# Depthwise-convolution taps issued between a mixer's attention units and gate blocks, one channel block wholly on Pool; rotary key rows kept in lasting tiles

## The chip, the cores and the metric

The kernel runs on one core of one Trainium2 chip (trn2). The metric is the device time of one execution in microseconds (us). TensorE (PE) multiplies; VectorE (DVE), ScalarE (ACT) and GpSimd (POOL) do everything else between its products; SyncE (SP) issues the weight loads.

## The reference, cut to what matters

The model is a two-layer hybrid block on 256 latent and 256 context tokens with 1024 channels. Each layer is a half-step feed-forward, a mixer, and a second half-step feed-forward. The change touches the mixer alone:

```python
def conv_module(zc, w_dw, b_dw, ln_g, ln_b, w_pw, b_pw):
    a, gt = jnp.split(zc, 2, axis=-1)
    v = a * jax.nn.sigmoid(gt)
    v = lax.conv_general_dilated(v, w_dw[:, None, :], window_strides=(1,),
                                 padding=[(CONV_K // 2, CONV_K // 2)],   # CONV_K = 31
                                 feature_group_count=CONV_CH) + b_dw     # CONV_CH = 384
    v = layer_norm(v, ln_g, ln_b)
    return jax.nn.silu(v) @ w_pw + b_pw
...
# every head's key: its own 64 rows, and 32 rotary rows shared by all 8 heads
k = jnp.concatenate([k_nope, jnp.broadcast_to(kr[:, :, None, :], (bsz, t, N_HEADS, QK_ROPE))], axis=-1)
...
g0, g1, g2 = jnp.split(jax.nn.sigmoid(u @ w_bg + b_bg), 3, axis=-1)
return (g0 * y_conv + g1 * y_mla + g2 * y_four) @ w_out
```

The second layer's mixer needs the latent stream only; its keys and values still come from both streams.

## The kernel before

Channels lie on the 128 partitions and tokens in the columns, latent and context side by side. Mixer 0 (layer 0) works on 512 columns; mixer 1 (the last layer) on 256, its keys on 512. A float32 product is made in three passes (L261 to L263) of split operands: high times high, high times low, low times high. Weights come as 512 KB tiles of 128x1024 on SP's queue into `raw` (3 buffers). ACT casts each to `wh` (L240), DVE subtracts to get the rest `wl` (L241); both have 5 buffers. PE's third pass (L263) is the one that reads `wl`.

A tile scheduler lays each engine's instructions out in program order with priorities, and each engine runs its own list in that order. `issue_after(x)` adds an ordering edge: what is emitted inside stands behind x. Tiles come from one pool by tag, each tag with a number of buffers (`BUFS`); a new tile of a full tag waits until the oldest one is no longer read.

A mixer runs in this order: the input projection; the norms and the rotary key rows (`rope_keys`); attention; the Fourier branch (`project`, `over_tokens`, `over_channels`); then the three branches by their gates, `wf` (Fourier, gate 2), `wo` (attention, gate 1), `pw` (convolution, gate 0), each in 8 output blocks m; then the output projection. One output block of `wf` or `wo` is 8 gate products and 4 branch products of three passes each, 36 matmuls on 12 weight blocks, which is one and a half weight tiles.

Attention goes in units of 128 queries of one head and stream: 32 units in mixer 0 (half of them with 512 keys, half with 256), 16 in mixer 1. For a unit, PE makes the scores, DVE takes the maximum (L762), ACT the exponentials (L765), DVE the reciprocal of their sum (L767), POOL multiplies (L768: the softmax product). PE transposes the unit's probabilities (L780) four units later. Keys are made per pair of heads into a fresh `kq` tile each, and POOL copies the shared rotary rows into it (L815, two copies a head).

The convolution has 31 taps for each of 3 channel blocks. A tap on DVE is one instruction that multiplies and adds (L669). A tap on POOL is two, a product into a scratch tile (L666) and an addition (L667). Before, blocks 0 and 1 run on DVE and block 2 on POOL; in mixer 1 POOL also takes 20 taps of block 1. All stand behind attention, two steps at a time around the parts of the Fourier branch, three per block of `wf`, and the rest at block 2 of `wo`, where the convolution's layer norm (`conv_norm`) starts. POOL's scratch tiles have the tag `hid`, which holds nearly every other 128x512 tile of the mixer too, also the 8 sums of the branches (`macc`), written by L1023.

Of the kernel before, what the change touches and what calls it, by code (L numbers as in the profile page):

```python
# [182 lines left out]
class Kern:  # L183
    def __init__(self, ctx, tc, nc, ap, offs):
        self.tc, self.nc, self.ap, self.offs = tc, nc, ap, offs
        pool = lambda name, bufs, **k: ctx.enter_context(tc.tile_pool(name=name, bufs=bufs, **k))  # noqa: E731
# [193 lines left out]
    def ada_steps(self, todo):  # L380
        """The adaLN vectors (layer, index) of todo, 128 channels a step: a row's products with silu(c), summed."""
        nc = self.nc
        cb = []
# [798 lines left out]
```

## Time and profile before

| | |
|---|---|
| three runs | 2027.84 us median, 2027.41 to 2029.29 |
| profiled execution | span 2026.3 us |
| PE, DVE, ACT, POOL busy | 97%, 64%, 37%, 18% of the span |
| tensor clock granted | 1.00 nearly throughout, less in a few stretches of the two mixers |
| mixer 0: attention, Fourier, `wf` and `wo` | about 477 to 545, 545 to 578, 578 to 700 us |
| mixer 1: the same | about 1611 to 1653, 1653 to 1680, 1680 to 1745 us |

All times of the trace count from the start of the span. What one execution takes beside its span is 1.5 us if the median stands for it. The windows give, for a stretch, how long each engine was busy, how many instructions it ran, and the clock that PE was granted as a share of full speed (2.4 GHz). A wait names the engine that stood still, the line that came next, and what released it.

### The profile page before, as it was taken

What the parts mean: (1) busy time and instruction counts of PE and PEld (TensorE: products, weight loads), DVE (VectorE), ACT (ScalarE), POOL (GpSimd) and SP (SyncE); (2) the same over time, 40 slices, a digit from 0 to 9 for tenths busy, and PEclk for the clock granted to TensorE, in tenths of its full rate; (3) what the DMA queues carried; (4) which work ended last, traced back from release to release, by engine and by line L of the source; (5) the groups of instructions that cost most, each with busy time, mean ns of one, the idle gap of its engine ahead of it and who ended that gap; (6) DMA issues with size and microseconds to landing.
All of it is one profiled execution on the core that took longest, in us unless ns stands there. A gap on an engine that the chain in (4) does not pass through costs nothing.

```text
span 2026.3 us, 27858 instructions
## 1 busy us (share of the span) xinstructions
PE 1971.3 (97%) x10949; PEld 1701.1 (84%) x10949; DVE 1287.2 (64%) x2064; ACT 759.0 (37%) x1171; POOL 361.3 (18%) x417
## 2 busy tenths in 40 slices
PE   7999999999979999999999999999999999899998
PEld 5888888988768888988888898888889878799997
DVE  5667667855698545666755766454456777577674
ACT  4322222345622434422132242222234663455453
POOL 1000000123686000100000010000001389300000
PEclk9999999999999999999999999999999999899999
DMA  9445545420213333444544534454542314465653
GB/s 351 158 163 190 175 158 179 133 94 22 71 42 125 94 104 112 139 151 152 183 159 147 168 120 160 166 187 145 166 141 88 105 60 148 135 198 178 184 181 102
DMA packets 81428, 290.44 MB, mean 143 GB/s; under 512 B 9232, under 2 KB 10512, under 8 KB 81296
## 3 DMA queue, kind: packets, MB, share of 16 engines
q1 hardware_dynamic: 62320, 221.01, 33.0%
q0 software_dynamic: 18432, 67.12, 10.7%
q8 instruction: 86, 1.41, 0.3%
q10 hardware_dynamic: 544, 0.52, 0.1%
q14 instruction: 46, 0.38, 0.1%
HBM read 287.57 MB, written 1.05 MB: 142 GB/s over the span
## 4 chain that ended last, share of the span: by engine, by line
PE 81%; issue 10%; POOL 5%; DVE 3%; ACT 1%; DMA 1%; SPq 0%; POOLq 0%; DVEq 0%; ACTq 0%
PE mm L261 25%; PE mm L263 25%; PE mm L262 25%; POOL hid L666 2%; POOL hid L667 2%; DVE hid L669 1%; PE mm L446 1%; PE mm L793 1%; PE mm L780 1%; PE mm L307 1%; DVE wl L241 1%; PE mm L320 1%; PE mm L939 1%; PE mm L458 0%; DVE hid L289 0%
## 5 line engine op out<-in xcount | busy, mean ns | idle before, releaser
L240 ACT CAST wh<-raw 128x1024 fp32r<-128x1024 f32 x394 | 412.9, 1050 | 1010.5 <-PE mm L262 606.6
L263 PE MATMUL mm<-uh,wl 128*128 128x512 f32 (+2 forms) x2056 | 717.1, 349 | 14.6 <-DVE wl L241 14.6
L261 PE MATMUL mm<-uh,wh 128*128 128x512 f32 (+2 forms) x2056 | 718.8, 350 | 0.0
L262 PE MATMUL mm<-ul,wh 128*128 128x512 f32 (+2 forms) x2056 | 716.9, 349 | 1.2 <-POOL ul L371 1.2
L241 DVE TENSOR_TENSOR wl<-raw,wh 128x1024 fp32r<-128x1024 f32 x394 | 494.2, 1256 | 255.7 <-ACT wh L240 255.2
L263 PEld LDWEIGHTS mm<-uh,wl 128*128 128x128 f32 x2056 | 392.3, 191 | 65.4 <-DVE wl L241 17.0
L262 PEld LDWEIGHTS mm<-ul,wh 128*128 128x128 f32 x2056 | 392.5, 191 | 51.0 <-POOL ul L371 1.4
L261 PEld LDWEIGHTS mm<-uh,wh 128*128 128x128 f32 x2056 | 392.0, 191 | 49.2 <-issue 1.0
L263 PE MATMUL mm<-hid,wl 128*128 128x512 f32 (+1 forms) x1086 | 372.9, 344 | 5.9 <-DVE wl L241 5.9
L261 PE MATMUL mm<-hid,wh 128*128 128x512 f32 (+1 forms) x1086 | 374.0, 344 | 0.0
L262 PE MATMUL mm<-hid,wh 128*128 128x512 f32 (+1 forms) x1086 | 372.8, 343 | 0.0
L398 DVE SCALAR_TENSOR_TENSOR kq<-kq,kq 128x1024 f32<-128x1024 f32 x224 | 273.0, 1219 | 1.3
L263 PEld LDWEIGHTS mm<-hid,wl 128*128 128x128 f32 x1086 | 206.4, 190 | 30.6 <-DVE wl L241 6.7
L261 PEld LDWEIGHTS mm<-hid,wh 128*128 128x128 f32 x1086 | 206.4, 190 | 24.5
L262 PEld LDWEIGHTS mm<-hid,wh 128*128 128x128 f32 x1086 | 206.4, 190 | 24.4
L396 POOL DMA_DIRECT2D kq<-in_ada x128 | 68.1, 532 | 890.3 <-DVE kq L398 804.0
L612 DVE TENSOR_TENSOR tmp<-mm,tmp 128x512 f32<-128x512 f32 (+1 forms) x70 | 46.2, 660 | 195.0 <-PE mm L263 195.0
L522 DVE SCALAR_TENSOR_TENSOR h<-mm,mod,h 128x256 f32<-128x256 f32 x136 | 61.4, 480 | 84.8 <-PE mm L263 84.4
L666 POOL TENSOR_SCALAR hid<-cv,vec,zero 128x251 f32<-128x251 f32 (+29 forms) x80 | 101.1, 1268 | 26.7 <-PE mm L262 15.2
L667 POOL TENSOR_TENSOR hid<-hid,hid 128x251 f32<-128x251 f32 (+29 forms) x80 | 89.2, 1116 | 1.7
L669 DVE SCALAR_TENSOR_TENSOR hid<-cv,vec,hid 128x482 f32<-128x482 f32 (+29 forms) x100 | 83.9, 882 | 0.2
L312 POOL TENSOR_TENSOR r<-ms,mhalf 128x2 f32<-128x2 f32 (+1 forms) x17 | 16.8, 987 | 362.2 <-DVE ms L310 362.2
(176 smaller groups left out, 1514.3 us busy)
## 6 DMA issues: line engine op xcount, KB each, us to landing
raw<-in_w SPq DMA_DIRECT2D x392, 512.0 KB, 4.1
kq<-in_ada POOLq DMA_DIRECT2D x128, 512.0 KB, 3.9
kq<-in_ada_first SPq DMA_DIRECT2D x16, 512.0 KB, 7.7
kq<-in_crow SPq DMA_DIRECT2D x6, 512.0 KB, 6.2
h<-in_xt SPq DMA_DIRECT2D x8, 256.0 KB, 4.1
raw<-in_four SPq DMA_DIRECT2D x2, 384.0 KB, 3.0
out_t<-hid ACTq DMA_DIRECT2D x2, 256.0 KB, 2.3
out_t<-hid SPq DMA_DIRECT2D x2, 256.0 KB, 2.4
```

What stands on the lines that cost most here:

```text
L240: a = nc.scalar.copy(out=wh, in_=raw)
L241: b = nc.vector.tensor_sub(out=wl, in0=raw, in1=wh.bitcast(F32))
L261: nc.tensor.matmul(out, lh, rh, start=k == 0, stop=False)
L262: nc.tensor.matmul(out, lh, rl, start=False, stop=False)
L263: nc.tensor.matmul(out, ll, rh, start=False, stop=k == n - 1)
L396: nc.gpsimd.dma_start(out=raw, in_=self.ap[f"ada{l}"][p - (2 if l == 0 else 0), b])
L398: nc.vector.scalar_tensor_tensor(out=junk, in0=raw, scalar=1.0, in1=cb[s], op0=ALU.mult, op1=ALU.mult, accum_out=m[:, s, b : b + 1])
L522: self.mark = self.nc.vector.scalar_tensor_tensor(out=h[:, cs], in0=ps, scalar=gate[:, s, kb : kb + 1], in1=h[:, cs], op0=ALU.mult, op1=AL ...
L612: self.mark = nc.vector.tensor_tensor(out=t, in0=p3[:, :n], in1=t, op=ALU.mult)
L666: nc.gpsimd.tensor_scalar(out=tmp, in0=src, scalar1=c, scalar2=self.zero, op0=ALU.mult, op1=ALU.add)
L667: nc.gpsimd.tensor_add(out=dst, in0=dst, in1=tmp)
L669: nc.vector.scalar_tensor_tensor(out=dst, in0=src, scalar=c, in1=dst, op0=ALU.mult, op1=ALU.add)
```

## The change

- The taps are two generators now, `near` (blocks 0 and 1, on DVE) and `far` (block 2, on POOL) in both mixers: 62 DVE taps and 31 POOL steps each. The 20 taps of block 1 that POOL had in mixer 1 are DVE's.
- They are called from inside attention by `during(i)`, behind unit i's scores. In mixer 1 each unit gets one DVE tap behind its maximum and one POOL step behind its softmax product. In mixer 0 every fourth unit gets a DVE tap, every second unit a POOL step. The 15 POOL steps left follow the last softmax product at once.
- None stands around the Fourier branch. The DVE taps left go 5 (mixer 0) or 4 (mixer 1) to an output block of `wf` and of `wo`, behind the block's product with its gate; `conv_norm` starts at block 3 or 4 of `wo`.
- POOL's scratch has a tag of its own, `ptmp`, with two buffers.
- `rope_keys` makes four lasting key tiles (`kt`) with the rotary rows in them, by 6 POOL copies ahead of attention; heads use them in turn, and the 16 copies of L815 are gone. `kq` has 4 buffers and not 6; the adaLN steps take their broadcast rows from `kt`. The scratch for POOL's DMA descriptors is set to 4096 bytes.

```diff
-    BUFS = {"hid": 26, "kq": 6, "tmp": 6, "cv": 3, "sq": 6}
+    BUFS = {"hid": 26, "kq": 4, "kt": 4, "tmp": 6, "cv": 3, "sq": 6, "ptmp": 2}
...
-                tmp = grid(self.blk("hid"))[:, :, lo:hi]
+                tmp = grid(self.blk("ptmp"))[:, :, lo:hi]
...
-        help_with = [(2, k) for k in order] + [(1, k) for k in order[late:]]
-        for i, k in enumerate(order):
-            tap(0, k, False)
-            if i < late:
-                tap(1, k, False)
-            while len(help_with) > (CONV_K - 1 - i) * (CONV_K + moved) // CONV_K:
-                tap(*help_with.pop(0), True)
-            yield
+        def steps(blocks, helper):
+            for k in order:
+                for j in blocks:
+                    tap(j, k, helper)
+                    yield
+
+        return steps((0, 1), False), steps((2,), True)
...
+        for to in kt[1:]:
+            for dst, src in zip(to, kr):
+                nc.gpsimd.tensor_scalar(
+                    out=dst[NOPE:], in0=src[NOPE:].bitcast(F32), scalar1=self.one[NOPE:], scalar2=self.zero[NOPE:], op0=ALU.mult, op1=ALU.add
+                )
+        return kt
...
-                kh, kl = self.pair()
+                kh, kl = kt[(2 * pr + hh) % 4]
                 self.split_from(pk[hh * NOPE : (hh + 1) * NOPE], kh[:NOPE], kl[:NOPE])
-                for dst, src in zip((kh, kl), kr):
-                    nc.gpsimd.tensor_scalar(
-                        out=dst[NOPE:], in0=src[NOPE:].bitcast(F32), scalar1=self.one[NOPE:], scalar2=self.zero[NOPE:], op0=ALU.mult, op1=ALU.add
-                    )
...
-        nc.vector.reduce_max(out=nb, in_=ps[:, :nk], axis=mybir.AxisListType.X, negate=True)
+        self.top = nc.vector.reduce_max(out=nb, in_=ps[:, :nk], axis=mybir.AxisListType.X, negate=True)
...
-        nc.gpsimd.tensor_scalar(out=p, in0=p, scalar1=ri, scalar2=self.zero, op0=ALU.mult, op1=ALU.add)
+        self.soft = nc.gpsimd.tensor_scalar(out=p, in0=p, scalar1=ri, scalar2=self.zero, op0=ALU.mult, op1=ALU.add)
...
                 self.scores(u)
+                each(i)
...
+        near, far = self.conv_steps(l, v, conv, ns)
+
+        def taps(n, ins):
+            with self.tc.issue_after(ins):
+                for _ in range(n):
+                    next(near, None)
+
+        per_m, at_m = (4, 4) if last else (5, 3)
+
+        def during(i):
+
+            taps(1 if last else i % 4 // 3, self.top.ins)
+            if last or i % 2:
+                with self.tc.issue_after(self.soft.ins):
+                    next(far, None)
...
+        with self.tc.issue_after(self.soft.ins):
+            for _ in far:
+                pass
...
-        taps(2)
         project(2)
-        taps(2)
         project(3)
-        taps(2)
         spectra = [over_tokens(b) for b in batches]
-        taps(2)
...
-        def normalise(m):
-            if m == 2:
-                taps(100)
+        def normalise(m, ins):
+            if m < at_m:
+                taps(per_m, ins)
+            elif m == at_m:
+                taps(100, ins)
                 self.conv_norm(l, conv, ns, y)
 
-        branch("wf", 2, four, self.vec(l, "b_four"), step=lambda m: taps(3))
+        branch("wf", 2, four, self.vec(l, "b_four"), step=lambda m, ins: taps(per_m, ins))
```

POOL's list at the first units of mixer 0's attention, before: L768 is the softmax product, L815 the copy of rotary rows.

```order
L768 TENSOR_SCALAR tmp_3758<-tmp_3758,ri_3761,zero 128x512
L768 TENSOR_SCALAR tmp_3776<-tmp_3776,ri_3779,zero 128x512
L815 TENSOR_SCALAR kq_3830<-hid_3439,one,zero 64x512
L768 TENSOR_SCALAR sq_3788<-sq_3788,ri_3791,zero 128x256
L768 TENSOR_SCALAR sq_3800<-sq_3800,ri_3803,zero 128x256
L815 TENSOR_SCALAR kq_3830<-hid_3440,one,zero 64x512
L768 TENSOR_SCALAR tmp_3812<-tmp_3812,ri_3815,zero 128x512
```

The same place of the changed kernel, where L774 is the softmax product and L664 with L665 one tap of block 2:

```order
L774 TENSOR_SCALAR tmp_3763<-tmp_3763,ri_3766,zero 128x512
L774 TENSOR_SCALAR tmp_3781<-tmp_3781,ri_3784,zero 128x512
L661 TENSOR_SCALAR hid_3665<-cv_3455,vec_94 128x512
L774 TENSOR_SCALAR sq_3794<-sq_3794,ri_3797,zero 128x256
L774 TENSOR_SCALAR sq_3806<-sq_3806,ri_3809,zero 128x256
L664 TENSOR_SCALAR ptmp_3813<-cv_3455,vec_94,zero 128x2x241
L665 TENSOR_TENSOR hid_3665<-hid_3665,ptmp_3813 128x2x241
L774 TENSOR_SCALAR tmp_3822<-tmp_3822,ri_3825,zero 128x512
```

The copies between the softmax products are gone, and a tap of two instructions stands behind every second product; the product that follows waits on POOL for both.

DVE's list at the last units of mixer 1's attention, before (L762 maximum, L767 reciprocal):

```order
L762 TENSOR_REDUCE nb_13180<-mm_13176 128x1
L762 TENSOR_REDUCE nb_13198<-mm_13194 128x1
L767 RECIPROCAL ri_13185<-sm_13183 128x1
L762 TENSOR_REDUCE nb_13217<-mm_13213 128x1
L767 RECIPROCAL ri_13203<-sm_13201 128x1
L767 RECIPROCAL ri_13222<-sm_13220 128x1
```

And of the changed kernel (L768 maximum, L773 reciprocal, L667 a tap):

```order
L768 TENSOR_REDUCE nb_13201<-mm_13197 128x1
L667 SCALAR_TENSOR_TENSOR hid_12664<-cv_12454,vec_95,hid_12664 128x246
L768 TENSOR_REDUCE nb_13223<-mm_13219 128x1
L773 RECIPROCAL ri_13206<-sm_13204 128x1
L667 SCALAR_TENSOR_TENSOR hid_12663<-cv_12453,vec_95,hid_12663 128x247
L768 TENSOR_REDUCE nb_13246<-mm_13242 128x1
L773 RECIPROCAL ri_13228<-sm_13226 128x1
```

One tap now stands between a unit's maximum and its reciprocal.

DVE's list in mixer 1's Fourier branch, before (L289 takes the low part of a split that PE's next product reads):

```order
L289 TENSOR_TENSOR hid_13390<-mm_13232,hid_13389 128x512
L669 SCALAR_TENSOR_TENSOR hid_13311<-cv_12461,vec_95,hid_13311 128x247
L669 SCALAR_TENSOR_TENSOR hid_13312<-cv_12462,vec_95,hid_13312 128x247
L669 SCALAR_TENSOR_TENSOR hid_13311<-cv_12461,vec_95,hid_13311 128x248
L669 SCALAR_TENSOR_TENSOR hid_13312<-cv_12462,vec_95,hid_13312 128x248
L669 SCALAR_TENSOR_TENSOR hid_13311<-cv_12461,vec_95,hid_13311 128x249
L289 TENSOR_TENSOR kq_13407<-mm_13408,kq_13406 128x512
```

And of the changed kernel, from the Fourier branch into the first block of `wf` (L1034 is the block's product with its gate):

```order
L289 TENSOR_TENSOR hid_13491<-tmp_13486,hid_13490 128x512
L241 TENSOR_TENSOR wl_13662<-raw_13659,wh_13661 128x1024
L289 TENSOR_TENSOR hid_13506<-tmp_13501,hid_13505 128x512
L241 TENSOR_TENSOR wl_13686<-raw_13683,wh_13685 128x1024
L1034 SCALAR_TENSOR_TENSOR hid_13509<-mm_13550,vec_95,tmp_13548 128x256
L667 SCALAR_TENSOR_TENSOR hid_12663<-cv_12453,vec_95,hid_12663 128x248
L667 SCALAR_TENSOR_TENSOR hid_12664<-cv_12454,vec_95,hid_12664 128x248
L667 SCALAR_TENSOR_TENSOR hid_12663<-cv_12453,vec_95,hid_12663 128x249
L667 SCALAR_TENSOR_TENSOR hid_12664<-cv_12454,vec_95,hid_12664 128x249
L241 TENSOR_TENSOR wl_13737<-raw_13734,wh_13736 128x1024
```

No tap stands among the splits any more; they follow a block's own product, four at a time, and the weight splits stand between.

## Rows read from the trace of the kernel before

**Rows 1.** Windows of mixer 0 (Fourier 560, branches 580).

```profile
core 0: us, PE busy (x) PEld busy (x) DVE busy (x) ACT busy (x) POOL busy (x), PEclk, DMA share, GB/s
440.00:460.00 20.00, 20.00 (x90) 16.57 (x89) 8.59 (x10) 7.00 (x9) 4.94 (x4) 1.00 0.35 107
480.00:532.00 52.00, 51.84 (x315) 41.19 (x314) 36.09 (x85) 40.54 (x110) 28.12 (x41) 1.00 0.10 29
560.00:580.00 20.00, 17.72 (x107) 15.33 (x108) 19.62 (x29) 7.02 (x15) 14.16 (x10) 1.00 0.00 1
580.00:620.00 40.00, 32.65 (x124) 25.56 (x123) 40.00 (x36) 8.27 (x9) 39.68 (x24) 0.87 0.31 92
```

**Rows 2.** Windows of mixer 1, same columns.

```profile
1611.00:1646.00 35.00, 33.45 (x207) 26.99 (x207) 24.75 (x55) 26.22 (x62) 22.10 (x26) 1.00 0.09 27
1660.00:1680.00 20.00, 16.50 (x89) 15.20 (x88) 17.02 (x30) 6.66 (x12) 19.84 (x23) 0.74 0.17 49
1680.00:1750.00 70.00, 55.16 (x399) 53.42 (x399) 45.56 (x59) 24.30 (x33) 60.18 (x65) 0.90 0.46 145
1750.00:1790.00 40.00, 40.00 (x335) 39.94 (x334) 28.11 (x49) 22.91 (x35) 1.63 (x1) 1.00 0.56 172
```

**Rows 3.** Waits of 575 to 620: us, times, longest.

```profile
PE mm L263 <- DVE wl L241: 8.7, 4, 4.1
```

**Rows 4.** Waits of 1690 to 1760, same columns.

```profile
DVE hid L1023 <- POOL hid L667: 20.7, 4, 7.3
PE mm L263 <- DVE wl L241: 10.8, 5, 4.0
```

**Rows 5.** Groups of 590 to 620: busy, mean ns.

```profile
L669 DVE SCALAR_TENSOR_TENSOR hid<-cv,vec,hid 128x508 f32<-128x508 f32 (+7 forms) x19 | 21.5, 1189 | 0.0
L666 POOL TENSOR_SCALAR hid<-cv,vec,zero 128x510 f32<-128x510 f32 (+8 forms) x9 | 16.9, 1881 | 0.0
L667 POOL TENSOR_TENSOR hid<-hid,hid 128x510 f32<-128x510 f32 (+7 forms) x9 | 14.9, 1655 | 0.3
```

**Rows 6.** Pool's tap pairs, 533 to 585: ns min/median/max.

```profile
L666 POOL TENSOR_SCALAR hid<-cv,vec,zero x14: 739/1670/2517, 533.5 to 581.8; 128x482 f32<-128x482 f32 x1, 128x484 f32<-128x484 f32 x1, 128x486 f32<-128x486 f32 x1, 128x488 f32<-128x488 f32 x1
L667 POOL TENSOR_TENSOR hid<-hid,hid x13: 1212/1555/2192, 536.7 to 583.5; 128x482 f32<-128x482 f32 x1, 128x484 f32<-128x484 f32 x1, 128x486 f32<-128x486 f32 x1, 128x488 f32<-128x488 f32 x1
```

**Rows 7.** The same of mixer 1, 1646 to 1742.

```profile
L666 POOL TENSOR_SCALAR hid<-cv,vec,zero x50: 544/752/2640, 1647.1 to 1736.6; 128x251 f32<-128x251 f32 x4, 128x252 f32<-128x252 f32 x4, 128x253 f32<-128x253 f32 x4, 128x254 f32<-128x254 f32 x4
L667 POOL TENSOR_TENSOR hid<-hid,hid x50: 692/731/1712, 1648.2 to 1739.1; 128x251 f32<-128x251 f32 x4, 128x252 f32<-128x252 f32 x4, 128x253 f32<-128x253 f32 x4, 128x254 f32<-128x254 f32 x4
```

**Rows 8.** A DVE tap: timeline at 558; group of 1680 to 1750.

```profile
558.47 0.71 DVE L669 SCALAR_TENSOR_TENSOR hid<-cv,vec,hid 128x490 f32<-128x490 f32 x1
L669 DVE SCALAR_TENSOR_TENSOR hid<-cv,vec,hid 128x251 f32<-128x251 f32 x1 | 0.5, 474 | 0.0
```

**Rows 9.** POOL groups of attention, 477 to 533.

```profile
L768 POOL TENSOR_SCALAR tmp<-tmp,ri,zero 128x512 f32<-128x512 f32 x16 | 12.3, 770 | 47.4 <-DVE ri L767 43.3 <-PE mm L263 3.5
L768 POOL TENSOR_SCALAR sq<-sq,ri,zero 128x256 f32<-128x256 f32 x16 | 8.8, 556 | 10.1 <-DVE ri L767 9.8
```

**Rows 10.** DVE groups of the same stretch.

```profile
L241 DVE TENSOR_TENSOR wl<-raw,wh 128x1024 fp32r<-128x1024 f32 x4 | 5.3, 1334 | 1.0 <-ACT wh L240 1.0
L289 DVE TENSOR_TENSOR kq<-tmp,kq 128x512 fp32r<-128x512 f32 x7 | 4.8, 687 | 1.1 <-ACT kq L288 1.1
```

**Rows 11.** Timeline: two softmax products, the transposes of the first.

```profile
486.42 1.13 POOL L768 TENSOR_SCALAR sq<-sq,ri,zero 128x256 f32<-128x256 f32 x2 [0.95 <-DVE ri L767]
490.26 0.38 PE L780 MATMUL mm<-ident,sq 128*128 128x128 f32 x2
```

**Rows 12.** Timeline of mixer 1's attention: POOL and DVE.

```profile
1624.42 2.11 POOL L768 TENSOR_SCALAR tmp<-tmp,ri,zero 128x512 f32<-128x512 f32 x1
1624.67 1.21 DVE L241 TENSOR_TENSOR wl<-raw,wh 128x1024 fp32r<-128x1024 f32 x1
```

**Rows 13.** Waits of 0 to 60 on SP's queue.

```profile
SPq L453 <- PE mm L458: 14.8, 9, 5.0
```

More of the change, by code (lines that the diff above doesn't have):

```diff
@@ L384, in ada_steps @@
         for s in (LAT, CTX):
-            t = self.blk("kq", (P, D))
+            t = self.blk("kt", (P, D))
             nc.sync.dma_start(out=t, in_=self.ap["crow"][s : s + 1, :].to_broadcast([P, D]))
@@ L389, in ada_steps @@
             nc.scalar.activation(out=t, in_=t, func=AF.Silu)
-        junk = self.blk("kq", (P, D))
+        junk = self.blk("kt", (P, D))
         for l, p in todo:
@@ L653, in conv_steps @@
         order = [mid] + [k for k in range(CONV_K) if k != mid]
-        moved = 20 if ns == 1 else 0
-        late = CONV_K - moved
         def tap(j, k, helper):
@@ L746, in rope_keys @@
         nc.vector.tensor_add(out=f[lo, :S], in0=f[lo, :S], in1=t[lo, :])
-        kr = self.blk("hid", dt=F32R), self.blk("hid", dt=F32R)
+        kt = []
+        for _ in range(4):
+            t = self.blk("kt", (P, 2, T), F32R)
+            kt.append((t[:, 0], t[:, 1]))
+        kr = kt[0]
         for rows in (lo, hi):
@@ L796, in values, with attention @@
         self.split_from(po[:, :S], u["o"][0][:, cs], u["o"][1][:, cs])
-    def attention(self, l, last, streams, cols, kvn, cqn, kr, vals, first, fill, ahead):
+    def attention(self, l, last, streams, cols, kvn, cqn, kt, vals, first, fill, ahead, each):
         nc = self.nc
@@ L900, in mixer @@
         cqn = self.lora_norm(l, cq, "g_q", ns * S, "q")
-        kr = self.rope_keys(self.zproj(l, "kr", full))
+        kt = self.rope_keys(self.zproj(l, "kr", full))
         v = [self.blk("cv") for _ in range(3)]
@@ L943, in project @@
                     self.split_from(zt[tb], *zs[tb])
-        att = self.attention(l, last, streams, cols, kvn, cqn, kr, vals, value_rows, [lambda: project(0), lambda: project(1)], (l, "z_f", 0))
         conv = [self.blk("hid") for _ in range(3)]
-        cst = self.conv_steps(l, v, conv, ns)
-        def taps(n):
-            for _ in range(n):
-                next(cst, None)
+        near, far = self.conv_steps(l, v, conv, ns)
[9 more added lines that the diff above has]
+                    next(far, None)
+        att = self.attention(l, last, streams, cols, kvn, cqn, kt, vals, value_rows, [lambda: project(0), lambda: project(1)], (l, "z_f", 0), during)
+        with self.tc.issue_after(self.soft.ins):
+            for _ in far:
+                pass
         fw = self.const_split(0, 2 * S + 2 * P)
@@ L997, in mixer @@
             nc.scalar.activation(out=warm, in_=self.zero, func=AF.Sigmoid)
-        taps(2)
         project(2)
-        taps(2)
         project(3)
-        taps(2)
         spectra = [over_tokens(b) for b in batches]
-        taps(2)
         for x in spectra:
             over_channels(*x)
-        taps(2)
         macc = [self.blk("hid") for _ in range(KD)]
@@ L1022, in branch @@
                 if bias is not None:
-                    nc.vector.scalar_tensor_tensor(out=dst, in0=py[:, cols], scalar=bias[:, m : m + 1], in1=gt, op0=ALU.add, op1=ALU.mult)
+                    mark = nc.vector.scalar_tensor_tensor(out=dst, in0=py[:, cols], scalar=bias[:, m : m + 1], in1=gt, op0=ALU.add, op1=ALU.mult)
                 else:
-                    nc.vector.tensor_tensor(out=dst, in0=py[:, cols], in1=gt, op=ALU.mult)
+                    mark = nc.vector.tensor_tensor(out=dst, in0=py[:, cols], in1=gt, op=ALU.mult)
                 if gi != 2:
@@ L1171 @@
     arrays, offs = _host_arrays(i)
-    nc = bacc.Bacc("TRN2", target_bir_lowering=False, num_devices=1)
+    nc = bacc.Bacc("TRN2", target_bir_lowering=False, num_devices=1, dynamic_dma_scratch_size=4096)
     ap = {}
```

3 lines of the change are left out of this document (1 added, 2 removed).

## The prediction

> **What bounds the kernel now.** I read the windows first. Where nothing disturbs it, PE is busy throughout: 20.00 of 20 us with 90 matmuls of 512 columns, 40.00 of 40 with 335 of 256 [rows 1, 2]. That gives the pitch of a product, 20/90 = 0.222 us and 40/335 = 0.119 us, and with it a way to price a bad stretch: the matmuls that are missing in it times the pitch, which counts idle time and clock together. The reader is to see two bad stretches, both where the taps stand now.
>
> Mixer 0, 580 to 620: 124 matmuls where 180 fit, so 56 x 0.222 = **12.4 us** lost. DVE is busy 40.00 of 40 and the clock is 0.87, between the two levels of 1.2 and 2.4 GHz [rows 1]. The waits name it: PE's third pass waits 8.7 us for `wl`, which queues on DVE behind taps [rows 3].
>
> Mixer 1, 1680 to 1750: 399 where 70/0.119 = 586 fit, so 187 x 0.119 = **22.3 us**. There DVE is not full (45.56 of 70) and POOL is (60.18) [rows 2]. DVE waits 20.7 us, four times, at L1023 for a `hid` tile that POOL's L667 still reads, and PE waits 10.8 us for the `wl` queued behind L1023 [rows 4]. So in mixer 1 it is the shared tag, not DVE's work, that starves PE. The Fourier branch ahead of it, 1660 to 1680, has 3.5 us of idle PE and a clock of 0.74 over the 16.5 busy us, some 16.5 x 0.26 = 4.3 us more: **7.8 us** [rows 2]. In mixer 0 the Fourier branch has 20 - 17.72 = **2.3 us** of idle [rows 1].
>
> All that the change can give back is 12.4 + 22.3 + 7.8 + 2.3 = 44.8 us.
>
> **What comes back.** *Mixer 0's gate blocks.* A block has 36 matmuls, 36 x 0.222 = 8.0 us. DVE then has five taps at 0.71 [rows 8], one and a half weight splits at 1.21 [rows 12] and the block's own product, which I price as a tap: 3.6 + 1.8 + 0.7 = 6.1 us, 76% of the block. POOL's remaining 15 steps end before this stretch (below), so the taps cost 0.71 and not the 1.19 that they take beside POOL [rows 5]. I take 12 of 12.4. *Fourier branches.* Taps no longer stand among the splits that PE's next product reads, but POOL's 15 leftover steps run beside them: 1.5 of 2.3 and, with a clock that recovers only partly, 5.5 of 7.8. *Mixer 1's gate blocks.* With POOL's scratch apart, no DVE instruction waits for POOL, and POOL has no work left here. A block lasts 36 x 0.119 = 4.3 us; DVE has four taps at 0.474 [rows 8], 1.8 us of splits and a product like a tap: 4.2 us, 98%. In `wo` an addition more makes it 4.6, for four blocks. I take 20 of 22.3, and 1 us of cost below for the four. Sum: 12 + 1.5 + 5.5 + 20 = **39 us** (30 to 44).
>
> **What it costs in attention.** POOL's softmax products stand between PE's scores and PE's transposes. In mixer 0 they take 12.3 + 8.8 = 21.1 us [rows 9]; the copies of rotary rows go. Added are one first tap (0.77, as a softmax product) and 15 steps of L664 and L665. The quickest pair of before took 0.739 + 1.212 = 1.95 us [rows 6], so 21.1 + 0.8 + 29.3 = 51.2 us of work on POOL in a stretch of about 52: full, if nothing slows it. PE is busy 51.84 of those 52 us [rows 1], so all lateness beyond the slack is PE's. The slack is at least 3.3 us: a product that ends at 486.42 + 0.56 is transposed at 490.26 [rows 11].
>
> Something does slow it. In 590 to 620, with DVE on taps and splits throughout, a pair took 1.881 + 1.655 = 3.54 us, and the DVE taps 1.19 for 0.71 [rows 5, 8]. A single instruction shows the same: a softmax product took 2.11 us, for 0.77, beside a weight split of 1.21 [rows 12, 9]. In attention DVE runs such work for 8 taps x 0.71 + 7 x 0.69 + 4 x 1.33 = 15.8 us, 30% of the stretch [rows 8, 10]. At 30% of the lengthening a pair takes 1.95 + 0.3 x 1.59 = 2.43 us and POOL has about 21.1 x 1.3 + 0.8 + 36.5 = 64.7 us. That is 12.7 too late at the end, 9 after the slack. The last units' transposes have project(0) and project(1) between them, so I take **6 us**. Bounds: 0, and with every pair at 3.54 21.1 + 0.8 + 53.1 - 52 - 3.3 = 20 us.
>
> In mixer 1 POOL has 16 x 0.77 + 0.6 + 15 x (0.544 + 0.692) = 31.4 us in 35 [rows 7, 2]. Beside the taps of before, 49 pairs took 1736.6 - 1647.1 = 89.5 us, 1.83 each [rows 7], which would make it 12.3 + 0.6 + 27.4 = 40.3. DVE, 24.75 busy in the 35 [rows 2], gets 16 x 0.474 = 7.6 more and is at 92%, with a tap between a unit's maximum and its reciprocal. Half way between the two prices POOL has 36, and DVE's delays come on top: **4 us** (0 to 8).
>
> The row says that each side is stretched. The Trainium skill ("SBUF — State Buffer", section "SBUF: two separate sides") has it harder: a DVE instruction with two SBUF inputs and a GpSimd instruction take the shared ports as an exclusive lock for the whole instruction, and the loser fully blocks. The trace agrees on the contention, not wholly on the lock: in 590 to 620 the quickest durations add up to 9 x 1.95 + 19 x 0.71 = 31.1 us without the splits, in 30 us. By the lock the sum would be 2007 us; by the row it is that below.
>
> **The other costs.** `conv_norm` starts one or two blocks later. Its steps are spaced by some 21,000 columns of products in the program, 82 x 0.119 = 9.8 us in mixer 1; three blocks of `wo` (12.9 us) cover that. If they did not, the norm's end would hold PE by what is missing; I take 1 (0 to 3). The near-full DVE in `wo`: 1 (0 to 4; five `wl` buffers are the cover). The lead-in's loads now reuse a tile four back rather than six. SP's queue waits there 14.8 us in 9 waits, 1.6 each [rows 13], so two buffers fewer may be two waits more, 3.3; I take 0.5, since they wait ahead of PE's need. At mixer 0's end two adaLN loads stand ahead of norm products on POOL; priced as one such wait, 1 (0 to 3). The six copies ahead of attention replace the four to six that stood there: 0. The smaller descriptor scratch: 0, since POOL's loads wait for DVE in the feed-forwards and not for each other; if that cover were gone, again a wait of 1.6.
>
> **The sum.** 6 + 4 + 1 + 1 + 0.5 + 1 = 13.5 us of cost against 39: 2026.3 - 39 + 13.5 = 2000.8 us of span, plus the 1.5 us by which the median of the runs (2027.84) lies above the span: **2002 us**.
>
> **The rivals.**
>
> *Attention becomes POOL's* (slower). Every pair costs what it did beside a full DVE: 20 us in mixer 0, 8 in mixer 1. Idle PE also costs clock: in 580 to 620 7.35 us idle went with 32.65 x 0.13 = 4.2 us of clock [rows 1]. So 28 x 1.57 = 44, and 3.5 of other costs: 2027.8 - 39 + 47.5 = 2036 us. For it speaks that POOL is at 98% even at its best price; against it that DVE's colliding work is 30% there, not 100%, and that mixer 1's attention had 1.55 us of idle at a clock of 1.00 [rows 2]. It decides from 35.5/1.57 = 23 us of idle PE in the two attentions.
>
> *Attention hides it all* (faster). The pairs take 1.95 and 1.24, and the lag of four units swallows the rest: 39 - 3.5 gained, 1992 us. For it speaks the slack of 3.3 us at each unit; against it the 2.11 us of one softmax product.
>
> *POOL waits whole instructions.* Mixer 0's POOL has 51.2 + 15.8 = 67 us, so 67 - 52 - 3.3 = 11.7 rather than 6: 2007 to 2008 us. It is the rule of the lock above.
>
> *Only the wait for scratch goes.* DVE at 98 to 107% in mixer 1's blocks leaves `wl` late: half of 22.3 and of the 5.5 come back, 11 + 3 + 13.5 = 27.5 of gain, 14 of cost: 2014 us. For it speaks that DVE gains 20 taps; against it that 20.7 us of its time were waiting.
>
> *Nothing gained.* Attention costs some 20 us with its clock and half of mixer 1 stays: within 4 us of 2028.
>
> **How the numbers follow.** Chances: the likeliest 0.40 (1996 to 2007 by its bounds of cost), attention free 0.20, lock 0.08, only the scratch 0.12, POOL-bound 0.13, nothing 0.07. The range that leaves out the last two, 0.20, is 1988 to 2020: 1988 is 44 of gain with 4 of cost, 2020 the scratch case with 6 more in attention. 0.2%, about 4 us, is what a measurement of this kernel can tell from no change; faster 0.40 + 0.20 + 0.08 + 0.12 = 0.80, same 0.07, slower 0.13.
>
> **What the profile after would show.** Right: no wait of DVE for a POOL tap; 90 matmuls per 20 us from 580 on and 85 per 10 us in mixer 1's blocks, clock 1.00; small waits of PE's transposes for POOL's softmax products, some 6 and 4 us; mean POOL pairs near 2.4 and 1.5 us in attention. Wrong: waits of L786 for L774 of over 20 us, a clock under 1.00 in attention, or `wl` still late behind L667.

## The result and the profile after

The changed kernel takes 1994.2 us (median; 1993.84 to 1996.49), beside 2028.57 us for the kernel before in the same runs: ratio 0.9834, interval 0.982 to 0.9847, some 34 us. Forecast were 2002 us and a range of 1988 to 2020. The profiled execution has a span of 1991.3 us, 35.0 less than before, and PE is busy 98% of it.

Both kernels, and all that follow, have 10949 matmuls in nearly one order, so a stretch can be timed from the start of one product to the start of another, by their number. I use these (times of before): lead-in, up to product 450 (73.5 us); mixer 0's attention with the first projections, 2390 to 2800 (480.6 to 552.7); its Fourier branch, to 2900 (570.3); its `wf` and `wo` with the norm, to 3300 (675.1); the end of the mixer, 4050 to 4200 (826.9 to 845.9); mixer 1's attention, 7960 to 8260 (1608.8 to 1660.4), Fourier branch, to 8400 (1687.8), blocks, to 8760 (1752.0), and convolution norm, to 8900 (1769.1). The other stretches between products agree within 0.3 us in all kernels; the first product starts at 11.0 to 13.0 us, and 7.05 to 7.75 us lie behind the last one's start. One profile stands behind each row. In before, e1 and e5 the convolution norm's first products stand ahead of product 8760, so that a wait for them counts to the blocks; in all others they stand behind it.

| kernel | lead-in | att 0 | Four 0 | blocks 0 | end 0 | att 1 | Four 1 | blocks 1 | norm 1 |
|---|---|---|---|---|---|---|---|---|---|
| before | 62.19 | 72.15 | 17.63 | 104.79 | 19.01 | 51.54 | 27.41 | 64.27 | 17.05 |
| after | 63.78 | 76.63 | 15.15 | 90.58 | 20.15 | 53.49 | 20.79 | 43.20 | 17.32 |
| e1 own scratch | 61.34 | 72.19 | 21.41 | 104.21 | 19.01 | 51.70 | 28.90 | 61.40 | 17.05 |
| e2 near out | 65.38 | 75.17 | 15.14 | 90.58 | 20.15 | 50.82 | 20.65 | 43.20 | 18.78 |
| e3 far out | 63.12 | 74.72 | 15.15 | 91.59 | 20.14 | 51.85 | 21.00 | 43.20 | 18.96 |
| e4 far double | 63.32 | 105.66 | 15.15 | 90.58 | 20.15 | 71.49 | 19.83 | 43.20 | 17.31 |
| e5 scratch, share | 62.69 | 72.14 | 21.98 | 103.23 | 19.02 | 51.68 | 32.61 | 49.16 | 17.05 |
| e6 Fourier taps | 62.70 | 75.13 | 21.40 | 92.53 | 20.14 | 50.83 | 25.11 | 44.72 | 17.40 |
| e7 silu late | 63.09 | 73.52 | 15.15 | 90.73 | 21.69 | 53.51 | 20.55 | 43.20 | 17.32 |
| e8 all out | 63.95 | 74.38 | 15.15 | 91.33 | 20.14 | 50.58 | 20.99 | 48.45 | 22.07 |
| e9 edges | 62.63 | 73.51 | 15.15 | 90.72 | 18.99 | 53.51 | 20.71 | 43.20 | 17.31 |
| e10 no kt | 61.35 | 83.14 | 15.15 | 90.73 | 18.99 | 61.08 | 21.31 | 43.20 | 17.30 |
| e11 hid scratch | 62.70 | 76.52 | 18.41 | 90.63 | 20.15 | 53.59 | 22.00 | 43.20 | 17.31 |
| e12 combined | 61.48 | 72.92 | 15.15 | 91.80 | 18.98 | 50.83 | 20.53 | 43.20 | 18.91 |

From before to after the Fourier branches and blocks give 2.5 + 14.2 + 6.6 + 21.1 = 44.4 us. The attentions take back 4.5 and 1.95, the lead-in 1.6, mixer 0's end 1.15, the norm 0.3: 9.5 together.

The windows of after (columns as in [rows 1]; mixer 1's lie where its attention, Fourier branch and blocks are now):

```profile
480.00:532.00 52.00, 49.98 (x295) 38.38 (x294) 42.05 (x89) 43.64 (x103) 48.13 (x50) 1.00 0.16 49
580.00:620.00 40.00, 40.00 (x178) 33.14 (x177) 30.53 (x39) 10.17 (x12) 5.48 (x4) 1.00 0.35 105
...
1602.00:1638.00 36.00, 33.39 (x204) 26.21 (x203) 33.43 (x70) 25.80 (x60) 32.67 (x40) 1.00 0.09 27
1651.00:1671.00 20.00, 18.05 (x128) 16.46 (x127) 16.25 (x22) 10.38 (x17) 19.61 (x21) 1.00 0.54 167
1671.00:1717.00 46.00, 46.00 (x386) 46.00 (x385) 42.09 (x74) 20.57 (x27) 3.85 (x4) 1.00 0.58 181
```

Against [rows 1, 2]: 178 matmuls stand where 124 stood, DVE has 30.53 of 40 us where it had all 40, and the clock is 1.00. Mixer 1's blocks are full. POOL has moved: 48.13 of 52 us in mixer 0's attention, before 28.12. PE waits there for little (waits of after on PE, 470 to 560; those of 575 to 800 are none):

```profile
PE mm L261 <- ACT kq L288: 1.5, 1, 1.5
PE mm L786 <- POOL sq L774: 1.2, 2, 0.9
```

POOL's groups of 479 to 540 answer to [rows 5, 9]:

```profile
L665 POOL TENSOR_TENSOR hid<-hid,ptmp 128x482 f32<-128x482 f32 (+13 forms) x14 | 19.1, 1362 | 1.0
L774 POOL TENSOR_SCALAR tmp<-tmp,ri,zero 128x512 f32<-128x512 f32 x16 | 15.5, 973 | 36.2 <-DVE ri L773 36.2
L664 POOL TENSOR_SCALAR ptmp<-cv,vec,zero 128x482 f32<-128x482 f32 (+13 forms) x14 | 11.8, 842 | 0.0
L774 POOL TENSOR_SCALAR sq<-sq,ri,zero 128x256 f32<-128x256 f32 x15 | 11.2, 753 | 0.0
L661 POOL TENSOR_SCALAR hid<-cv,vec 128x512 f32<-128x512 f32 x1 | 1.0, 1044 | 0.0
```

A pair takes 0.842 + 1.362 = 2.20 us, and the softmax products 0.97 and 0.75 where they took 0.77 and 0.56: POOL is stretched beside DVE, by less than beside a DVE full of taps (3.54 a pair).

### The profile page after: what moved, and what is told of

The parts are those of the page before. It is cut to its first block, busy times and chain, and to the rows that moved or that the text cites. A ratio compares the mean times of both kernels' runs of the same rounds, so it can differ in the third digit from the quotient of the medians.

```text
span 1991.3 us, 27772 instructions
## 1 busy us (share of the span) xinstructions
PE 1955.0 (98%) x10949; PEld 1687.2 (85%) x10949; DVE 1271.1 (64%) x2084; ACT 758.9 (38%) x1171; POOL 289.6 (15%) x357
## 4 chain that ended last, share of the span: by engine, by line
PE 85%; issue 10%; POOL 2%; DVE 1%; DMA 1%; ACT 1%; SPq 0%; POOLq 0%; DVEq 0%; ACTq 0%
PE mm L261 27%; PE mm L263 27%; PE mm L262 27%; PE mm L942 1%; PE mm L446 1%; PE mm L799 1%; PE mm L307 1%; PE mm L320 1%; PE mm L786 0%; POOL sq L774 0%; POOL tmp L774 0%; PE mm L458 0%; POOL hid L665 0%; DMA raw<-in_w 0%; DVE wl L241 0%
## 5 line engine op out<-in xcount | busy, mean ns | idle before, releaser
L241 DVE TENSOR_TENSOR wl<-raw,wh 128x1024 fp32r<-128x1024 f32 x394 | 489.3, 1244 | 273.5 <-ACT wh L240 272.9
L398 DVE SCALAR_TENSOR_TENSOR kt<-kq,kt 128x1024 f32<-128x1024 f32 x224 | 272.9, 1218 | 1.3
L522 DVE SCALAR_TENSOR_TENSOR h<-mm,mod,h 128x256 f32<-128x256 f32 x136 | 61.3, 480 | 84.7 <-PE mm L263 84.3
L667 DVE SCALAR_TENSOR_TENSOR hid<-cv,vec,hid 128x482 f32<-128x482 f32 (+29 forms) x120 | 72.8, 655 | 0.0
L665 POOL TENSOR_TENSOR hid<-hid,ptmp 128x482 f32<-128x482 f32 (+29 forms) x60 | 68.0, 1133 | 3.3
L289 DVE TENSOR_TENSOR hid<-tmp,hid 128x512 fp32r<-128x512 f32 (+1 forms) x100 | 62.9, 629 | 2.2 <-ACT hid L288 1.9
```

The source lines that it names most:

```text
L241: b = nc.vector.tensor_sub(out=wl, in0=raw, in1=wh.bitcast(F32))
L289: self.nc.vector.tensor_sub(out=lo, in0=src, in1=hi.bitcast(F32))
L398: nc.vector.scalar_tensor_tensor(out=junk, in0=raw, scalar=1.0, in1=cb[s], op0=ALU.mult, op1=ALU.mult, accum_out=m[:, s, b : b + 1])
L522: self.mark = self.nc.vector.scalar_tensor_tensor(out=h[:, cs], in0=ps, scalar=gate[:, s, kb : kb + 1], in1=h[:, cs], op0=ALU.mult, op1=AL ...
L665: nc.gpsimd.tensor_add(out=dst, in0=dst, in1=tmp)
L667: nc.vector.scalar_tensor_tensor(out=dst, in0=src, scalar=c, in1=dst, op0=ALU.mult, op1=ALU.add)
```

## The experiments

**Where the taps stand: e1 to e4.** The first asks whether the shared tag was the cause in mixer 1. It also sets the scratch for POOL's DMA descriptors to 4096 bytes, as the changed kernel does; so does e5.

```diff
 kernel before
-                tmp = grid(self.blk("hid"))[:, :, lo:hi]
+                tmp = grid(self.blk("ptmp"))[:, :, lo:hi]
```

> The kernel before with POOL's scratch in a tag of its own and nothing else moved. Theory A (mixer 1's loss is DVE standing at L1023 for POOL's scratch): the 20.7 us wait goes, about half of mixer 1's 22.3 us comes back, mixer 0 stays as it was: 2014 us (2008 to 2020). Theory B (what counts is where the taps stand, the tag only names the wait): POOL still ends its 101 instructions near 1740 and DVE waits for it at the end instead: 2024 to 2030 us.

2029.82 us, ratio 1.0008 (0.9998 to 1.0017): nothing gained, as theory B has it. Waits of 1655 to 1765, and two windows:

```profile
DVE tmp L687 <- POOL hid L667: 15.8, 1, 15.8
...
PE mm L699 <- DVE tmp L688: 15.2, 1, 15.2
```

```profile
1690.00:1730.00 40.00, 40.00 (x334) 40.00 (x334) 34.41 (x41) 20.06 (x26) 39.37 (x36) 0.99 0.69 215
1730.00:1750.00 20.00, 4.76 (x24) 4.38 (x23) 4.23 (x9) 2.08 (x5) 13.19 (x22) 0.62 0.11 33
```

The 20.7 us of [rows 4] are gone and PE runs through the blocks. Then it reaches the convolution norm, whose sum (L687) reads POOL's last tap, and stands. The wait for scratch was a symptom: POOL's 101 instructions are not done before about 1740 either way. And both Fourier branches got slower (17.63 to 21.41, 27.41 to 28.90).

Next, each kind of tap out of attention, and POOL's doubled there:

```diff
 e2: changed kernel
-            taps(1 if last else i % 4 // 3, self.top.ins)
-        per_m, at_m = (4, 4) if last else (5, 3)
+        per_m, at_m = (6, 4) if last else (6, 3)
 e3: changed kernel
-            if last or i % 2:
-                with self.tc.issue_after(self.soft.ins):
-                    next(far, None)
 e4: changed kernel
                     next(far, None)
+                    next(far, None)
```

> The changed kernel without DVE taps in attention; they go six to an output block. The alignment of both traces gives 4.5 us lost in mixer 0's attention and 1.95 in mixer 1's. Theory A (late POOL softmax products are what attention loses): these stay within 1 us, and mixer 1's blocks, with six taps at 5.1 us of DVE against 4.3 of PE, lose up to 8: about 2001 us. Theory B (DVE's taps delay the query splits and slow POOL): attention loses under 2 us in both together, so about 1996 to 1998 us with the same loss in the blocks.

> The changed kernel with all 31 POOL steps behind the last softmax product, DVE taps where they are. Theory A (POOL steps in attention cost the 4.5 and 1.95 us, but running them beside the blocks' DVE taps costs more): attention's loss falls under 1.5 us, and POOL's steps reach into four or five blocks of wf in both mixers, where DVE needs 8.9 of 8.0 us and 5.7 of 4.3 us a block: about 1998 us. Theory B (steps beside the gate blocks are hidden since PE waits for nothing there): 1988 us.

> The changed kernel with two POOL steps wherever attention had one, so that all 31 stand inside attention. Theory A (POOL is full there: a pair more costs its whole length): 15 x 2.2 = 33 us in mixer 0 and 15 x 1.57 = 24 in mixer 1, together 57 us, and more if the clock falls with the idle time: 2050 to 2080 us. Theory B (POOL has room, the 6.4 us are DVE's): under 20 us more, below 2014 us.

e2: 1991.49 us, ratio 0.9814 (0.98 to 0.9829). Attention gains 1.5 us in mixer 0 and 2.7 in mixer 1, and the blocks lose nothing, though DVE is full there (window of its blocks in mixer 1):

```profile
1669.00:1714.00 45.00, 45.00 (x378) 45.00 (x377) 44.97 (x87) 18.98 (x25) 2.79 (x3) 1.00 0.50 156
```

Only the norm behind them comes 1.5 us later. My price of 8 us in the blocks is refuted, and with it the times of both theories. e3: 1993.0 us, 0.9823 (0.9809 to 0.9838): 1.9 and 1.6 us gained in the attentions, 1.0 lost in mixer 0's blocks and 1.6 at mixer 1's norm. Neither theory's figure; steps outside cost less than A said and more than B. Taken together, e2 and e3 say that in mixer 1 neither kind of tap alone is the price: without DVE's taps attention is 2.7 us shorter, without POOL's steps 1.6, and the whole loss was 1.95. e4: 2039.43 us, 1.0051 (1.0036 to 1.0066): attention 29.0 and 18.0 us longer for some 15 pairs each. Those are 15 x 2.20 = 33 and 15 x 1.57 = 24 us of POOL at the means in the changed kernel (the 1.57 is 0.73 + 0.84, its pair in mixer 1). Theory A in kind: POOL has little room left, and past it PE pays 88% and 75% of the added pairs. The 45 us lost are under the 57 that theory A named. PE's waits and the clock of e4 in mixer 0:

```profile
PE mm L786 <- POOL tmp L774: 12.1, 6, 4.1
PE mm L786 <- POOL sq L774: 5.7, 3, 3.3
```

```profile
480.00:520.00 40.00, 30.38 (x153) 23.14 (x152) 27.67 (x52) 22.67 (x59) 38.52 (x41) 0.89 0.05 14
520.00:570.00 50.00, 38.91 (x202) 28.78 (x200) 29.89 (x51) 31.82 (x68) 49.77 (x50) 0.91 0.22 70
```

**What the gain comes from: e5, e6, e8.** e5 is e1 with POOL's share of block 1 given back to DVE (`moved = 0`). e6 is e2 with 20 DVE taps put back around the Fourier branch, four at each of the five old places. e8 is the changed kernel with `during` empty and six taps a block.

> The kernel before with POOL's own scratch and, beside it, the 20 taps of block 1 given back to DVE; all taps stand where they stood. Theory C (mixer 1's loss was POOL's amount of work: with 61 instructions instead of 101 it ends near 1705, ahead of the convolution's norm): most of the blocks' loss comes back, some 20 us, the Fourier part stays: 2008 us (2003 to 2013). Theory D (the taps must also be spread over the blocks): DVE with six taps a block beside POOL is 7.2 us of work in a block of 4.3 and delays wl: 2016 to 2024 us.

> The changed kernel without DVE taps in attention, with 20 of them a mixer at the five places around the Fourier branch where they stood before, and six to a block until they run out; POOL's steps as in the changed kernel. It is to be compared with the run without DVE taps in attention (1991.5). Theory E (taps among the splits of the Fourier branch delay PE): 2 to 3 us lost in mixer 0's Fourier branch and 4 to 6 in mixer 1's, 1998 us. Theory F (they hurt only as long as POOL runs 31 or more steps beside them): within 1.5 us of 1991.5.

> The changed kernel with no tap in attention at all: 31 POOL steps behind the last softmax product, DVE's taps six to a block from the first block of wf, none around the Fourier branch. Theory I (the gain comes from POOL's smaller share and from the free Fourier branch, attention is needed for nothing): the losses in attention fall to those of ACT, the blocks lose little as in the two single steps: 1988 to 1992 us. Theory J (with both outside, DVE has six taps at 1.19 us, 2.6 of splits and 0.7 beside a busy POOL, 10.5 us in blocks of 8.0, as before): 12 us lost in mixer 0 and as many in mixer 1, 2010 us or more.

e5: 2020.51 us, ratio 0.9962 (0.9947 to 0.9977). Mixer 1's blocks give 15.1 of 21.1 us, 2.9 of them already in e1, so POOL's share is the larger part, as theory C has it (POOL's last tap ends at 1705.6); but the Fourier branches lose 4.4 and 5.2 and the time is theory D's. Window of mixer 1's Fourier branch in e5, and of mixer 0's in e6:

```profile
1665.00:1698.00 33.00, 25.98 (x146) 24.09 (x146) 30.92 (x46) 9.20 (x16) 32.29 (x36) 0.74 0.22 65
```

```profile
556.00:578.00 22.00, 19.32 (x103) 17.03 (x102) 21.28 (x28) 8.18 (x15) 21.69 (x17) 0.84 0.01 2
```

DVE and POOL both work with hardly a pause, PE idles between splits, and the clock is 0.74 and 0.84. Before, POOL stood 9.5 us in mixer 0's Fourier branch, waiting for a `hid` tile that PE still read (waits of before on POOL, 545 to 580; POOL was busy 14.16 of 20 us there [rows 1]):

```profile
POOL hid L666 <- PE mm L263: 9.5, 1, 9.5
```

With its own scratch it runs on, beside DVE's taps, and e1 and e5 lose time there.

e6: 2003.35 us, ratio 0.9881 (0.9866 to 0.9895), 11.9 us over e2: 6.3 and 4.5 us in the Fourier branches, 1.95 and 1.5 in the blocks behind them. Theory E, and double its price in mixer 0: the window has 2.7 us of idle PE and, at 0.84 over 19.32 busy us, 3.1 us of clock. Keeping the Fourier branch free of DVE taps is thus worth some 12 us.

e8: 1999.44 us, ratio 0.9859 (0.9844 to 0.9873). Mixer 0 loses nothing to speak of: blocks 0.75 us longer, attention 2.25 shorter. That is no light load there (window of e8):

```profile
590.00:620.00 30.00, 30.00 (x134) 24.85 (x133) 30.00 (x27) 7.11 (x9) 29.61 (x18) 1.00 0.22 70
```

DVE and POOL are as full as before the change (40.00 and 39.68 of 40 us [rows 1]), and still PE never stands. What differs is how DVE enters the blocks. Weight splits (L241) ended by the start of product 2920 number 89 in before, e1, e5 and e6, where DVE taps stand around the Fourier branch, and 92 in all others: a lead shorter by three `wl` tiles, of which there are five. The lost lead alone (e6, where POOL has few steps left) costs the blocks 1.95 us, a full POOL beside a full DVE alone (e8) 0.75; before had both and lost 14.2. The edge that holds taps behind a block's product is in e6 and e8 too; what it is worth by itself was not run. Mixer 1 loses 5.25 in the blocks and 4.75 at the norm. Neither I nor J as a whole: of the two mixers it is the last, with blocks half as long, that needs part of its taps in attention.

**What attention loses, and the key tiles: e7, e9, e10.** The trace of after showed something that no step of mine had (ACT's timeline):

```profile
515.75 1.28 ACT L389 ACT_TABLE_LOAD   x1
517.05 1.06 ACT L389 ACTIVATE kt<-kt 128x1024 f32<-128x1024 f32 x1
518.13 0.58 ACT L288 CAST kt<-mm 64x512 fp32r<-64x512 f32 x1
518.74 1.28 ACT L771 ACT_TABLE_LOAD   x1
520.03 0.69 ACT L771 ACTIVATE tmp<-mm,nb 128x512 f32<-128x512 f32 x1
520.62 0.19 ACT L771 ACTIVATION_READ_ACCUMULATOR tmp<-mm,nb 128x1 f32 x1
520.71 0.61 ACT L288 CAST kq<-tmp 128x512 fp32r<-128x512 f32 x1
```

L389 is the silu of an adaLN row for the second feed-forward. The rows live in `kt` tiles now. A `kt` tile comes free when the heads that used it are done, which is inside attention, and the scheduler put the silu there, between two table loads. The query split behind it is late, and PE with it (1.51 us at 521.37). A second one stands at 528.35. In before, both stand behind attention, at 755 and 760 us. e7 orders them behind the convolution norm's silu; e9 behind the next norm, with two edits more:

```diff
 e9: changed kernel
+            with self.tc.issue_after(self.uh_last.ins) if behind else contextlib.nullcontext():
                 nc.scalar.activation(out=t, in_=t, func=AF.Silu)
+                with self.tc.issue_after(self.ul_last.ins) if behind else contextlib.nullcontext():
                     nc.gpsimd.dma_start(out=raw, in_=self.ap[f"ada{l}"][p - (2 if l == 0 else 0), b])
...
-                raw = self.blk("kq", (P, D))
+                raw = self.blk("kq" if (4 * q + part) % 6 < 4 else "kt", (P, D))
 e10: the first two of these, and
-                kh, kl = kt[(2 * pr + hh) % 4]
+                kh, kl = self.pair()
...
+                for dst, src in zip((kh, kl), kt[0]):
+                    nc.gpsimd.tensor_scalar(
```

The last edit of e9 is in the lead-in's loads. `behind` is true for the adaLN rows of the second feed-forward of layer 0. e10 has five `kq` and three `kt` tiles.

> The changed kernel with one ordering edge more: the two silu of the adaLN rows, which now stand inside mixer 0's attention on ACT with a table load before and after each (7.2 us of ACT), go behind the convolution norm's own silu. Theory G (these hold up the query splits, and PE with them): mixer 0's attention loses 1.5 to 3 us less than the 4.5 of the changed kernel, 1991.5 to 1993 us. Theory H (ACT has room there, the loss is POOL's and DVE's): no difference, 1994.2 within 1 us.

> The changed kernel with three edits, each read in its own stretch. First, the two silu of the adaLN rows stand behind the last high part of the norm ahead of the second feed-forward, out of attention: mixer 0's attention 3 us shorter, as with the silu behind the convolution norm, and no loss at the mixer's end for it. Second, POOL's adaLN loads of that feed-forward stand behind the norm's last product on POOL: if their wait for kq tiles is what costs 1.15 us there, that stretch goes from 20.15 back to 19.0 us; if it is the smaller kq itself, it stays. Third, the lead-in's loads go round six tiles again (four kq, two kt): if the smaller kq costs the lead-in 1.6 us, it is 61.3 to 62.7 as in three kernels with six; if the lead-in only varies from run to run (61.3 to 65.4 so far), anything in that range. Together 1988 to 1990 us.

> The changed kernel with the first two of these edits and without lasting key tiles: every head's keys in a fresh kq tile with two POOL copies of the rotary rows, as before; 16 copies, 10 of them inside attention, 8.4 to 8.7 us of POOL. Theory A (POOL is nearly full in attention, 48.1 of 52 us busy in mixer 0): mixer 0's attention loses 5 to 9 us and mixer 1's 3 to 8 against the run with edges, some 2000 us. Theory K (POOL's lateness is hidden by the lag of four units): under 2 us in both together, 1990 us.

e7: 1992.11 us, ratio 0.982 (0.9803 to 0.9836). Mixer 0's attention is 3.1 us shorter (theory G), but the mixer's end takes 1.5 of that back. e9: 1988.12 us, ratio 0.9802 (0.9788 to 0.9817): the same 3.1 us, and the end at 18.99, as before. The 1.15 us there had been POOL's adaLN load, which stood for a `kq` tile ahead of the norm's product (L371; POOL's timeline of after):

```profile
811.74 0.64 POOL L396 DMA_DIRECT2D kq<-in_ada  x1 [3.81 <-PE mm L263]
812.85 0.54 POOL L396 DMA_DIRECT2D kq<-in_ada  x1 [0.47 <-PE mm L263]
813.78 0.74 POOL L371 TENSOR_TENSOR ul<-sq,uh 128x256 fp32r<-128x256 f32 x1 [0.40 <-ACT uh L370]
```

The lead-in took 62.63 us in e9 and 61.48 in e12, with six tiles in turn; kernels with five or six have 61.3 to 62.7, those with four 62.7 to 65.4. That fits some 1.5 us for the smaller `kq`, but the spread within a group is as large (1.4 and 2.7 us).

e10: 2005.05 us, ratio 0.9885 (0.9869 to 0.9902): without lasting key tiles the attentions are 9.6 and 7.6 us longer than in e9. Theory A, in mixer 0 a little over what it said. PE's waits of e10 in mixer 0's attention (L790 are the transposes, L778 the softmax products), 470 to 560, and the longest of mixer 1's, 1585 to 1660 (L825 are the copies):

```profile
PE mm L790 <- POOL tmp L778: 6.0, 3, 2.6
PE mm L790 <- POOL sq L778: 1.2, 2, 0.8
...
PE mm L263 <- POOL kq L825: 3.3, 3, 2.1
```

In mixer 1 PE's scores wait for the copies themselves, and inside attention no copy waits for a `kq` tile, so the five tiles are not what costs. So the key tiles are what makes the taps in attention affordable: together with the taps they are worth 17 us, half of the whole gain. The kernel before with the key tiles alone was not run.

**The scratch tag in the changed kernel: e11.** The changed kernel with `self.blk("hid")` for POOL's scratch again.

> The changed kernel with POOL's scratch back in the tag hid. If the gain rests on POOL ending ahead of the blocks, no tile waits for scratch any more and the time is that of the changed kernel, 1994 us within 2. If the tag itself matters, DVE waits for L665 in the blocks or POOL waits for hid tiles in attention: 2000 us or more.

1996.83 us, ratio 0.985 (0.9836 to 0.9865), between the two figures; its interval overlaps that of the changed kernel. The blocks are as they were (90.63, 43.20), so no tile waits there. The Fourier branches are 3.3 and 1.2 us longer in the one profile. In mixer 0's, PE stands 2.8 us, where it has no wait in after, for splits of ACT and DVE; ACT's order is another one (ACT's timelines of e11, first two lines, and of after):

```profile
563.87 1.04 ACT L240 CAST wh<-raw 128x1024 fp32r<-128x1024 f32 x1 [4.38 <-PE mm L942]
564.82 2.04 ACT L288 CAST hid<-mm 128x512 fp32r<-128x512 f32 x4
...
560.50 0.59 ACT L288 CAST hid<-mm 128x512 fp32r<-128x512 f32 x1 [0.30 <-PE mm L942]
```

In e11 four splits stand behind a weight cast that waits for PE, and come all at once; in after each follows its product. The tag is the only edit; why it moves the cast was not tried.

**Combined: e12.** The three edits of e9 with those of e2, five taps a block in mixer 1.

> The three edits and no DVE taps in attention: six to a block in mixer 0, five in mixer 1; POOL's steps stay in attention. By the stretches measured so far: attention 3 + 1.5 us shorter in mixer 0 and 2.7 in mixer 1, the mixer's end 1.15, the lead-in 0 to 1.6, the convolution norm of mixer 1 up to 1.5 longer: 1994.2 - 8 to 1994.2 - 9.5, about 1986 us (1984 to 1988). If DVE becomes the bound in the blocks instead, 1990 us or more.

1986.45 us (1985.91 to 1986.59), ratio 0.9794 (0.9779 to 0.9809): the fastest, some 8 us under the changed kernel. Attention has 72.92 and 50.83 us; mixer 1's norm is 1.6 us longer (e2: 1.5). Mixer 0's blocks are 1.2 us longer, which e2 with the same six taps does not have. It is not the taps, the first of which starts at 580.12. PE waits once, for a split behind a long weight split (DVE's and PE's timelines of e12):

```profile
574.31 2.26 DVE L242 TENSOR_TENSOR wl<-raw,wh 128x1024 fp32r<-128x1024 f32 x1
576.49 1.70 DVE L290 TENSOR_TENSOR hid<-tmp,hid 128x512 fp32r<-128x512 f32 x1
...
578.25 0.50 PE L263 MATMUL mm<-hid,wh 128*128 128x512 f32 x1 [0.92 <-DVE hid L290]
```

Against e9 the two intervals overlap: the edges are shown, a gain from DVE's taps out of attention on top of them is not.

## Why the prediction was right, and where not

**Mixer 0: direction and size right, the mechanism in part.** DVE fell from 40.00 to 30.53 of 40 us, PE's wait for `wl` went, and for the 12 and 1.5 us taken 14.2 and 2.5 came. The prediction had it that a lighter DVE gives them: five taps at 0.71 us, 76% of a block. But in e8 DVE is full, beside a full POOL, and the blocks lose 0.75 us. `wl` came late because DVE went into the blocks three splits behind, from the Fourier branch, and could not catch up beside POOL; taking away either one is nearly enough (e6, e8).

**Mixer 1: size right, reason wrong.** "It is the shared tag, not DVE's work, that starves PE" fell with e1: the tag alone gives nothing, the wait moves to the norm. Of the 21.1 us (20 taken), POOL's smaller share together with its own scratch gives 15.1 (e5; the scratch alone 2.9), and the rest goes with where the taps stand. The step that failed is reading a releaser as a cause: L1023's wait named the tile, and what kept the tile was POOL's backlog, 1647.1 to past 1739.1 [rows 7]. The forecast of this stretch held by luck, because the change took both away.

**The Fourier branches** gave 9.1 us for 7 taken; e6 shows them as the most sensitive place.

**Attention: 10 us taken, 6.4 measured, and the sum was made of the wrong parts.** Of mixer 0's 4.5 us, 3.1 are ACT's two silu (e7, e9), which no step foresaw, so late softmax products and DVE's taps cost 1.4, not 6. POOL's load was close: 64.7 us forecast; the groups above make 19.1 + 15.5 + 11.8 + 11.2 + 1.0 = 58.6, with the last product (2.30, below) 60.9, and with a fifteenth pair, which comes behind it, some 63. By the lock of the Trainium skill ("SBUF — State Buffer", section "SBUF: two separate sides") the estimate was 67, with all of DVE's 15.8 us added; the trace stands between that and the free 51.2. What failed is the slack. I took the smallest one, 3.3 us, for the last units; the last product ends at 541.87 + 2.30 = 544.17, and its transposes start at 544.23 (after), where before it ended at 532.75 and they started at 544.95 (after, then before):

```profile
541.87 2.30 POOL L774 TENSOR_SCALAR sq<-sq,ri,zero 128x256 f32<-128x256 f32 x1
544.23 0.33 PE L786 MATMUL mm<-ident,sq 128*128 128x128 f32 x1
...
531.65 1.10 POOL L768 TENSOR_SCALAR sq<-sq,ri,zero 128x256 f32<-128x256 f32 x2
544.95 0.44 PE L780 MATMUL mm<-ident,sq 128*128 128x128 f32 x2
```

Some 12 us of slack at the end took nearly all of the backlog; PE's waits for softmax products come to 1.2 us. In mixer 1, 4 us were taken and 1.95 measured. By e2 and e3 either kind of tap, taken out, gives most or all of it back; the prediction had put the price of one on top of the other's.

**The copies of rotary rows** had been passed over in a clause ("go"). e10 prices them at 17 us in company with the taps.

**The small costs.** The mixer's end: 1 taken, 1.15 measured, by the mechanism named (e9). Lead-in: 0.5 taken, about 1.5. The norm's later start and the near-full DVE: 2 taken, 0.3; in e2 even a DVE at 44.97 of 45 us delayed nothing in the blocks. Costs thus came to 9.5 for 13.5, gains to 44.4 for 39: the 9.5 us between the forecast span, 2000.8, and the measured one, 1991.3, are 5.4 of gain and 4.0 of cost.

**The rivals.** "Only the wait for scratch goes" rested on DVE being too full, which e2 refutes. "Attention becomes POOL's" did not come, but e4 shows what a POOL past its room costs: 2039 us. That this is near the rival's 2036 is chance, since e4 has more pairs and the rival had longer ones; there idle PE went with clocks of 0.89 and 0.91. The rival by the lock (2007 to 2008) used the same 3.3 us of slack, so the measured time says nothing about the lock. The time lies in the range but under the 1996 to 2007 of the case held likeliest, and closest to "attention hides it all" (1992), though attention did not hide it all.

## What to carry to other kernels

A wait names what is held, not why: ask what its holder does next, and who reads that last. A full engine is not yet a late one: look at the lead with which it enters a stage (e8, e6). Work moved under another stage cost little here as long as the engine there had room, and past that PE paid three quarters of it or more (e4), so count what else can leave that engine first. When a tile gets a new tag, look at what else uses the tag: its release can decide where a scheduler puts that work, and here a silu among exponentials brought two table loads of 1.28 us with it.

## What the runs showed of the hardware

A wait can protect: POOL's 9.5 us of standing still kept it off DVE in the Fourier branch, and with its own scratch (e1) the branch took 21.4 us for 17.6, the DVE taps of 553 to 575 took 1085 ns for 934 on average, and the clock of 556 to 575 was 0.82 for 1.00. And idle time of PE in attention went with different clocks: 2.0 us of 52 with 1.00 (after), 9.6 of 40 with 0.89 (e4).
